# The low parts of the split weight tiles: VectorE and GpSimd together, or VectorE alone

## The chip, the cores and the metric

The kernel runs on one core of a Trainium2 chip. What is compared is the device time of one execution in microseconds (us), as the median of several runs. Besides that there is one profiled execution, whose trace tells when each instruction began and ended on each engine: PE (TensorE matmuls, with PEld for the weight loads that overlap them), DVE (VectorE), ACT (ScalarE), POOL (GpSimd) and SP (SyncE, which here only issues DMAs).

## The reference, cut to what matters

Two layers of a hybrid backbone work on 256 context tokens and 512 latent tokens of width 1024. Each layer normalizes and modulates its input, makes one large input projection, feeds three parallel branches (SSD, gated linear attention GLA, and S5), and ends in an output projection and a residual.

```
u_lat = rmsnorm(h_lat, norm_w[l]) * (1.0 + scale[:, None]) + shift[:, None]
u_ctx = rmsnorm(h_ctx, norm_w[l]) * (1.0 + scale_c) + shift_c
(z_c, xbc_c, dt_c, q_c, k_c, v_c, gg_c, lr_c, u5_c, sg_c) = split_in_proj(u_ctx @ w_in[l])
(z_l, xbc_l, dt_l, q_l, k_l, v_l, gg_l, lr_l, u5_l, sg_l) = split_in_proj(u_lat @ w_in[l])
...
ssd_c, ssd_l = ssd_branch(...)
gla_c, gla_l = gla_branch(...)
s5_c, s5_l = s5_branch(...)
...
y = pr[..., :S5_WIDTH] * jax.nn.sigmoid(pr[..., S5_WIDTH:])      # in s5_branch, after y @ glu_w
```

All of it is in 32-bit floating point. The weight matrices that concern us are `w_in`, `w_out` and `glu_w`.

## The kernel before, in words

A 32-bit product is made of three faster ones. Each operand is split into a high part, rounded to the type `fp32r`, and a low part, which is the operand minus its high part. The matmuls then add high*high, high*low and low*high (`PASSES`). For a weight tile of 128 x 1024 the function `wsplit` does the splitting: a DMA brings the tile into `wr`, ACT copies it with rounding into `wh`, and one `tensor_tensor` with SUB makes `wl = wr - wh`. Each of the three tags has two buffers, so the next tile but one can be loaded only when the subtraction has read `wr`, and its `wh` written only when PE has read the old one. There are 122 weight tiles, two of them 128 x 512 (the `wdl` tile of each layer). They are used by `proj` (input projection; L492 makes the latent columns in a `pl` bank, L494 the context columns in `pc`), by the V projection (L709), by the GLU of S5 (L1026, L1028) and by `out_part` (L1062, L1064).

Which engine makes a low part is set by a counter: each third tile goes to VectorE (`V`), the others to GpSimd (`G`). So VectorE makes 40 and GpSimd 82. The parameter `eng` is given by no caller.

The order of instructions on each engine is not the order of the source. A scheduler simulates the program as it is built and issues each instruction on its engine's queue where its own estimate of times puts it; each queue is then worked off strictly in order. A change to one instruction can therefore move others.

Other places that the text speaks of: `s5_out_map` (L375 to L385 on POOL, matmuls L394, DVE L400 and L401) makes the S5 output maps, 16 per layer, between the projections; L473 on DVE makes the low parts of the normalized input; `carry` (L643 to L646) is the S5 scan on DVE; L830 and L833 finish the GLA branch on DVE and POOL; `conv_tile` (L856, L863, L865 on DVE) is the convolution; L916, L918 and L921 on DVE, with the copies on ACT and L941, L944 and L954 on POOL, are the SSD chunks; L511 on DVE is a gate that also empties a projection's PSUM bank; all ACT instructions have the line of their helper, L121.

Of the kernel before, what the change touches and what calls it, by code (L numbers as in the profile page):

```python
# [8 lines left out]
F32 = mybir.dt.float32  # L9
# [6 lines left out]
ADD, SUB, MUL, MIN, MAX = ALU.add, ALU.subtract, ALU.mult, ALU.min, ALU.max  # L16
# [25 lines left out]
def hybrid_backbone_kernel(  # L42
# [16 lines left out]
    V, S, G, PE = nc.vector, nc.scalar, nc.gpsimd, nc.tensor  # L59
# [9 lines left out]
    def T(tag, shape, bufs, dt=F32):  # L69
        uid[0] += 1  # L70
        return sb.tile(shape, dt, tag=tag, bufs=bufs, name=f"{tag}_{uid[0]}")
# [48 lines left out]
    def act(out, in_, f, **kw):  # L120
        return S.activation(out, in_, f, **kw)  # L121
# [282 lines left out]
        dma(gD[l][gs + 1], gt[48:64])  # L404


    wcount = [0]

    def wsplit(src, n=1024, eng=None):

        wr = T("wr", [128, 1024], 2)[:, :n]
        dma(wr, src)
        wh, wl = (T(t, [128, 1024], 2, F32R)[:, :n] for t in ("wh", "wl"))
        act(wh, wr, AF.Copy)
        wcount[0] += 1
        (eng or (V if wcount[0] % 3 == 0 else G)).tensor_tensor(wl, wr, wh.bitcast(F32), SUB)  # L416
        return wh, wl

    def split(hi, lo, x, eng):
# [56 lines left out]
    def layer(l, u):  # L476
# [5 lines left out]
        def proj(blocks, m=128, ctx_too=True, src=None, early=False):  # L482

            w = wsplit(src if src is not None else wblk[l, blocks], 8 * m)
            p_l, p_c = pl(), pc() if ctx_too else None
            seq = [(k, wi, ui) for k in range(8) for wi, ui in PASSES]
            if early:
                seq.sort(key=lambda a: a[2])
            for n, (k, wi, ui) in enumerate(seq):
                st, sp = n == 0, n == 23  # L490
                lhs = w[wi][:, k * m : (k + 1) * m]
                PE.matmul(p_l[:m], lhs, u[k][:, ui, LC:NT], start=st, stop=sp)  # L492
                if ctx_too:
                    PE.matmul(p_c[:m], lhs, u[k][:, ui, 0:LC], start=st, stop=sp)  # L494
            return p_c, p_l
# [204 lines left out]
        for hb in range(2):  # L700
            ws = [wsplit(wblk[l, BV + 2 * hb + i]) for i in range(2)]
            for c in range(6):
                if c % 3 == 0:
                    e_ = ev()
                p = pl()[:, 0:256]
                n = 0
                for k in range(8):
                    for wi, ui in PASSES:
                        PE.matmul(p, u[k][:, ui, 128 * c : 128 * c + 128],  # L709
                                  ws[k // 4][wi][:, 256 * (k % 4) : 256 * (k % 4) + 256], start=n == 0, stop=n == 23)  # L710
                        n += 1
                act(e_[:, 256 * (c % 3) : 256 * (c % 3) + 256], p, AF.Copy)
                if c % 3 == 2:
                    dma(vD[l][128 * c - 256 : 128 * c + 128, 256 * hb : 256 * hb + 256].rearrange("(c p) v -> p c v", c=3),
                        e_.rearrange("p (c v) -> p c v", c=3))
# [301 lines left out]
        for m in range(4):  # L1017
            wv = wsplit(wglu[l, m])
            pair = []
            for half in range(2):  # L1020
                p_l, p_c = pl(), None if last else pc()
                n = 0
                for k in range(4):
                    for wi, ui in PASSES:
                        lhs = wv[wi][:, (half * 4 + k) * 128 : (half * 4 + k) * 128 + 128]
                        PE.matmul(p_l, lhs, yg5[k][:, ui, LC:NT], start=n == 0, stop=n == 11)  # L1026
                        if not last:
                            PE.matmul(p_c, lhs, yg5[k][:, ui, 0:LC], start=n == 0, stop=n == 11)  # L1028
                        n += 1
                pair.append((p_c, p_l)[-len(cols):])  # L1030

            sg, gt = cv(NT), cv(NT)
            dma(gt[:, t0:NT], sgD[l][128 * m : 128 * m + 128, t0:NT])
            for i, (a, b) in enumerate(cols):
                act(sg[:, a:b], pair[1][i], AF.Tanh, scale=2.0, bias=pcol("glb", 8 * l + 4 + m))
            s3 = sg[:, t0:NT].rearrange("p (t c) -> p t c", t=8)
            V.scalar_tensor_tensor(s3, s3, 1.0, gt[:, t0:NT].rearrange("p (c t) -> p t c", t=8), ADD, MUL)
            for i, (a, b) in enumerate(cols):
                V.scalar_tensor_tensor(sg[:, a:b], pair[0][i], pcol("glb", 8 * l + m), sg[:, a:b], ADD, MUL)
            t = hl()  # L1040
            s3, hi, lo = (a.rearrange("p (c t) -> p c t", t=8) if k else a.rearrange("p (t c) -> p c t", t=8)
                          for k, a in enumerate((sg[:, t0:NT], t[:, 0, t0:NT], t[:, 1, t0:NT])))
            split(hi, lo, s3, G)
            ys5.append(t)
# [215 lines left out]
```

## Time and profile before

| what | value |
|---|---|
| median of 3 runs | 1697.27 us (1695.55 to 1711.04) |
| profiled execution, its own time | 1712.97 us |
| its span from first to last instruction | 1711.3 us |
| granted TensorE clock, mean over the span | 0.901 of full speed |

The profiled execution took 15.7 us more than the median. Sums made from its rows are differences against 1712.97 us, and are carried over to the median of 1697.27 us.

### The profile page before, as it was taken

What the parts mean: (1) busy time and instruction counts of PE and PEld (TensorE: products, weight loads), DVE (VectorE), ACT (ScalarE), POOL (GpSimd) and SP (SyncE); (2) the same over time, 40 slices, a digit from 0 to 9 for tenths busy, and PEclk for the clock granted to TensorE, in tenths of its full rate; (3) what the DMA queues carried; (4) which work ended last, traced back from release to release, by engine and by line L of the source; (5) the groups of instructions that cost most, each with busy time, mean ns of one, the idle gap of its engine ahead of it and who ended that gap; (6) DMA issues with size and microseconds to landing.
All of it is one profiled execution on the core that took longest, in us unless ns stands there. A gap on an engine that the chain in (4) does not pass through costs nothing.

```text
span 1711.3 us, 23539 instructions
## 1 busy us (share of the span) xinstructions
PE 1418.1 (83%) x8536; PEld 1145.2 (67%) x8536; DVE 1168.2 (68%) x1992; ACT 679.9 (40%) x1220; POOL 783.2 (46%) x716
## 2 busy tenths in 40 slices
PE   3867766888989779977779999997889989967886
PEld 2656655777966557755668786886678777745665
DVE  7977558995477567679994127289835986688752
ACT  4312223225342336646553124343345345545442
POOL 3615647632268843445463141164123323656454
PEclk9788987898988889988889999998988999988998
DMA  8474654332543354444455745522363242344542
GB/s 308 124 185 135 178 150 135 93 118 71 176 123 86 100 165 140 142 154 139 128 187 188 282 135 178 189 85 80 111 193 107 64 139 93 119 138 145 184 131 96
DMA packets 139885, 243.55 MB, mean 142 GB/s; under 512 B 31992, under 2 KB 72568, under 8 KB 139768
## 3 DMA queue, kind: packets, MB, share of 16 engines
q1 hardware_dynamic: 139768, 242.04, 45.3%
q8 instruction: 67, 1.10, 0.3%
q14 instruction: 50, 0.41, 0.1%
HBM read 192.81 MB, written 49.18 MB: 141 GB/s over the span
## 4 chain that ended last, share of the span: by engine, by line
PE 25%; DVE 18%; DMA 13%; POOL 6%; issue 4%; ACT 4%; SPq 0%; DVEq 0%; ACTq 0%; POOLq 0%
PE pl L492 7%; PE pl L1062 6%; DMA bA<-acsD 5%; DMA bB<-acsD 3%; PE pc L494 2%; PE pc L1064 2%; DVE xy L863 1%; DMA wr<-in_wblk 1%; ACT bA L121 1%; POOL wl L416 1%; DVE bB L916 1%; DVE bA L916 1%; DVE xy L645 1%; DMA cs<-zD 1%; DVE bA L644 1%
## 5 line engine op out<-in xcount | busy, mean ns | idle before, releaser
L492 PE MATMUL pl<-hl,wh 128*128 128x512 f32 (+1 forms) x1184 | 411.5, 414 | 15.9 <-DVE ev L511 12.3
L416 POOL TENSOR_TENSOR wl<-wr,wh 128x1024 fp32r<-128x1024 f32 (+1 forms) x82 | 210.4, 2566 | 308.5 <-ACT wh L121 284.6
L492 PEld LDWEIGHTS pl<-hl,wh 128*128 128x128 f32 (+1 forms) x1184 | 226.0, 195 | 73.5 <-DVE ev L511 13.6
L492 PE MATMUL pl<-hl,wl 128*128 128x512 f32 (+1 forms) x592 | 243.5, 412 | 20.0 <-POOL wl L416 10.7
L121 ACT ACTIVATE wh<-wr 128x1024 fp32r<-128x1024 f32 (+1 forms) x122 | 127.6, 1047 | 283.7 <-PE pc L1064 69.3
L494 PE MATMUL pc<-hl,wh 128*128 128x256 f32 (+1 forms) x864 | 202.0, 304 | 11.3 <-DVE ev L511 7.2
L494 PEld LDWEIGHTS pc<-hl,wh 128*128 128x128 f32 (+1 forms) x864 | 152.5, 202 | 26.1 <-DVE ev L511 8.7
L492 PEld LDWEIGHTS pl<-hl,wl 128*128 128x128 f32 (+1 forms) x592 | 115.4, 195 | 49.1 <-POOL wl L416 12.0
L494 PE MATMUL pc<-hl,wl 128*128 128x256 f32 (+1 forms) x432 | 128.6, 298 | 0.0
L1062 PE MATMUL pl<-hl,wh 128*128 128x512 f32 x256 | 87.7, 419 | 16.9 <-ACT hl L121 4.6
L394 PE MATMUL pa<-cs 64*32 64x128 f32 x512 | 42.9, 305 | 64.0 <-POOL cs L382 27.3
L494 PEld LDWEIGHTS pc<-hl,wl 128*128 128x128 f32 (+1 forms) x432 | 87.3, 202 | 2.7 <-issue 1.7
L121 ACT ACTIVATE ev<-pl 128x512 f32<-128x512 f32 (+1 forms) x96 | 51.1, 534 | 87.7 <-PE pl L709 43.9
L709 PE MATMUL pl<-wh,hl 128*128 128x256 f32 x384 | 79.6, 307 | 2.6 <-ACT ev L121 2.6
L416 DVE TENSOR_TENSOR wl<-wr,wh 128x1024 fp32r<-128x1024 f32 x40 | 55.4, 1386 | 38.3 <-ACT wh L121 38.1
L121 ACT ACTIVATE bB<-bB 128x512 f32<-128x512 f32 (+4 forms) x40 | 45.7, 1142 | 85.1 <-DMA bB<-acsD 52.3
L394 PEld LDWEIGHTS pa<-cs 64*32 64x32 f32 x512 | 21.5, 115 | 80.6 <-POOL cs L382 28.9
L863 DVE SCALAR_TENSOR_TENSOR xy<-ev,par_sb,xy 128x512 f32<-128x512 f32 (+1 forms) x112 | 74.8, 704 | 0.6
L375 POOL TENSOR_SCALAR cs<-cs 128x32 f32<-128x32 f32 x32 | 20.1, 629 | 118.4 <-DMA cs<-in_s5cb 43.3
L709 PEld LDWEIGHTS pl<-wh,hl 128*128 128x128 f32 x384 | 66.9, 214 | 7.8 <-ACT ev L121 3.8
L1062 PEld LDWEIGHTS pl<-hl,wh 128*128 128x128 f32 x256 | 49.8, 199 | 31.1 <-ACT hl L121 6.7
L709 PE MATMUL pl<-wl,hl 128*128 128x256 f32 x192 | 58.4, 308 | 3.8 <-DVE wl L416 3.8
(483 smaller groups left out, 3604.4 us busy)
## 6 DMA issues: line engine op xcount, KB each, us to landing
wr<-in_wblk SPq DMA_DIRECT2D x80, 512.0 KB
wr<-in_wout SPq DMA_DIRECT2D x32, 512.0 KB
hl<-in_mod_w SPq DMA_DIRECT2D x20, 512.0 KB
bA<-acsD SPq DMA_DIRECT2D x10, 1024.0 KB
bB<-acsD SPq DMA_DIRECT2D x10, 1024.0 KB
clD<-cs SPq DMA_DIRECT2D x64, 128.0 KB
cs<-clD SPq DMA_DIRECT2D x32, 256.0 KB
cs<-in_mod_w SPq DMA_DIRECT2D x16, 512.0 KB
```

Source lines behind the costliest of these rows:

```text
L121: return S.activation(out, in_, f, **kw)
L375: G.tensor_scalar(cn, cb[:, 0:32], -1.0, None, MUL)
L394: PE.matmul(pk[d][32 * gg : 32 * gg + 32], b0[64 * d : 64 * d + 64, a, :], w54[64 * d : 64 * d + 64, a, gg, d : 8 + d, :].rearrange("p k h ...
L416: (eng or (V if wcount[0] % 3 == 0 else G)).tensor_tensor(wl, wr, wh.bitcast(F32), SUB)
L492: PE.matmul(p_l[:m], lhs, u[k][:, ui, LC:NT], start=st, stop=sp)
L494: PE.matmul(p_c[:m], lhs, u[k][:, ui, 0:LC], start=st, stop=sp)
L644: V.tensor_tensor(tr[:, 1, :n], li, src[:, :, ::-1], MUL)
L709: PE.matmul(p, u[k][:, ui, 128 * c : 128 * c + 128], ws[k // 4][wi][:, 256 * (k % 4) : 256 * (k % 4) + 256], start=n == 0, stop=n == 23)
L863: V.scalar_tensor_tensor(ac, raw[:, o + k : o + k + n], pcol("cw", w0 + k), ac, MUL, ADD)
L916: V.scalar_tensor_tensor(rf[:, h, :], rbw[:, h, :], rb[:, ih : ih + 1], rf[:, h, :], SUB, MIN)
L1062: PE.matmul(p_l, lhs, rhs[kk][:, ui, LC - t0 : NT - t0], start=st, stop=sp)
L1064: PE.matmul(p_c, lhs, rhs[kk][:, ui, 0:LC], start=st, stop=sp)
```

## The change

The counter and the `eng` parameter go, and VectorE makes every low part.

```diff
--- before.py
+++ after.py
@@ -404,16 +404,13 @@
-    wcount = [0]
-
-    def wsplit(src, n=1024, eng=None):
+    def wsplit(src, n=1024):
 
         wr = T("wr", [128, 1024], 2)[:, :n]
         dma(wr, src)
         wh, wl = (T(t, [128, 1024], 2, F32R)[:, :n] for t in ("wh", "wl"))
         act(wh, wr, AF.Copy)
-        wcount[0] += 1
-        (eng or (V if wcount[0] % 3 == 0 else G)).tensor_tensor(wl, wr, wh.bitcast(F32), SUB)
+        V.tensor_tensor(wl, wr, wh.bitcast(F32), SUB)
         return wh, wl
```

The file is three lines shorter, so L416 of before is L413 after, and all later lines move by three. In the rows below, the numbers behind a name tell its instances apart and are the same in both kernels. On POOL, at the end of GLA in layer 0, two weight tiles' low parts stood among the instructions of `s5_out_map` (before):

```order
L383 TENSOR_TENSOR cs_2306<-s5p_1800,cs_2306 128x288
L375 TENSOR_SCALAR cs_2333<-cs_2333 128x32
L380 TENSOR_TENSOR cs_2333<-s5p_1800,cs_2333 128x288
L381 TENSOR_TENSOR cs_2333<-s5p_1800,cs_2333 128x288
L416 TENSOR_TENSOR wl_4870<-wr_4867,wh_4869 128x1024
L382 TENSOR_TENSOR cs_2306<-cs_2306 128x288
L383 TENSOR_TENSOR cs_2333<-s5p_1800,cs_2333 128x288
L833 TENSOR_TENSOR m_266_2994<-m_266_2994,bB_2995 128x3072
L382 TENSOR_TENSOR cs_2333<-cs_2333 128x288
L384 TENSOR_TENSOR cs_2306<-s5p_1800,cs_2306 128x288
L416 TENSOR_TENSOR wl_4946<-wr_4943,wh_4945 128x1024
```

On DVE, the first of the two stands after the change behind the GLA norm's large multiply (L827, which was L830) and inside one convolution tile:

```order
L827 SCALAR_TENSOR_TENSOR m_266_2994<-m_266_2994,par_sb,bB_2995 128x3072
L400 TENSOR_TENSOR cs_2090<-cs_2090,pa_2102 64x16
L860 SCALAR_TENSOR_TENSOR bc_4694<-ev_4693,par_sb,bc_4694 128x512
L860 SCALAR_TENSOR_TENSOR bc_4694<-ev_4693,par_sb,bc_4694 128x256
L401 SCALAR_TENSOR_TENSOR cs_2090<-i_96,par_sb,cs_2090 64x16
L413 TENSOR_TENSOR wl_4870<-wr_4867,wh_4869 128x1024
L860 SCALAR_TENSOR_TENSOR bc_4694<-ev_4693,par_sb,bc_4694 128x512
L860 SCALAR_TENSOR_TENSOR bc_4694<-ev_4693,par_sb,bc_4694 128x256
L862 SCALAR_TENSOR_TENSOR bc_4694<-ev_4693,bc_4694 128x512
```

So the subtraction no longer stands behind `s5_out_map` and the GLA gate's product (L833) on POOL; behind it now stand the last taps of the convolution tile.

At the start of layer 0, on DVE, the low parts of the normalized input (L473) are followed before by other small work:

```order
L473 SCALAR_TENSOR_TENSOR hl_457<-xy_141,modp,hl_457 128x512
L345 TENSOR_TENSOR cs_174<-s5p_139,cs_171 128x576
L210 TENSOR_TENSOR modp<-pa_420,par_sb 128x8
L261 COPY bA_484<-bA_484 128x32
L298 TENSOR_TENSOR bA_484<-bA_484 128x32
```

and after the change by the first two weight tiles' subtractions, which stood on POOL with nothing ahead of them but the normalization:

```order
L470 SCALAR_TENSOR_TENSOR hl_457<-xy_141,modp,hl_457 128x512
L345 TENSOR_TENSOR cs_174<-s5p_139,cs_171 128x576
L210 TENSOR_TENSOR modp<-pa_420,par_sb 128x8
L413 TENSOR_TENSOR wl_553<-wr_550,wh_552 128x512
L261 COPY bA_484<-bA_484 128x32
L298 TENSOR_TENSOR bA_484<-bA_484 128x32
L413 TENSOR_TENSOR wl_863<-wr_860,wh_862 128x1024
```

Here the first subtraction has come to stand behind eight of the sixteen L473 and L345, and the other eight L473 stand behind both. Over the whole program all 122 subtractions are on DVE, none on POOL, and the remaining instructions of each engine are the same but for four fewer table loads on ACT.

## Rows read from the trace of the kernel before

**Rows 1.** The page: each engine's busy time, share and instructions.

```profile
PE 1418.1 (83%) x8536; PEld 1145.2 (67%) x8536; DVE 1168.2 (68%) x1992; ACT 679.9 (40%) x1220; POOL 783.2 (46%) x716
```

**Rows 2.** The chain that ended last, by engine.

```profile
PE 25%; DVE 18%; DMA 13%; POOL 6%; issue 4%; ACT 4%; SPq 0%; DVEq 0%; ACTq 0%; POOLq 0%
```

**Rows 3.** Stretches: us; busy PE, PEld, DVE, ACT, POOL; clock, DMA.

```profile
650.00:700.00 50.00, 48.33 (x308) 39.68 (x307) 27.68 (x51) 36.75 (x81) 19.68 (x15) 1.00 0.27 88
950.00:1050.00 100.00, 96.58 (x621) 71.56 (x620) 34.12 (x57) 28.75 (x40) 24.04 (x14) 0.97 0.52 186
1140.00:1210.00 70.00, 56.83 (x338) 49.09 (x337) 69.06 (x93) 27.89 (x36) 28.61 (x16) 0.90 0.30 91
```

**Rows 4.** Line L416, its instructions: duration in ns, least, median, most.

```profile
L416 POOL TENSOR_TENSOR wl<-wr,wh x82: 1290/2400/5506, 46.4 to 1684.5; 128x1024 fp32r<-128x1024 f32 x80, 128x512 fp32r<-128x512 f32 x2
L416 DVE TENSOR_TENSOR wl<-wr,wh x40: 1207/1224/2489, 70.0 to 1673.6; 128x1024 fp32r<-128x1024 f32 x40
```

**Rows 5.** The page's group of L416 on DVE: busy, mean ns, idle before.

```profile
L416 DVE TENSOR_TENSOR wl<-wr,wh 128x1024 fp32r<-128x1024 f32 x40 | 55.4, 1386 | 38.3 <-ACT wh L121 38.1
```

**Rows 6.** Timeline: start, us, what; DVE instructions beside a subtraction on POOL.

```profile
45.85 4.95 DVE L473 SCALAR_TENSOR_TENSOR hl<-xy,modp,hl 128x512 fp32r<-128x512 f32 x3
46.45 3.80 POOL L416 TENSOR_TENSOR wl<-wr,wh 128x512 fp32r<-128x512 f32 x2 [9.23 <-ACT wh L121]
...
326.53 2.36 POOL L416 TENSOR_TENSOR wl<-wr,wh 128x1024 fp32r<-128x1024 f32 x1
326.76 2.94 DVE L646 TENSOR_TENSOR xy<-xy,bA 128x768 f32<-128x768 f32 x1
...
333.97 0.94 DVE L646 TENSOR_TENSOR xy<-xy,bA 128x768 f32<-128x768 f32 x1
...
1539.60 2.38 POOL L416 TENSOR_TENSOR wl<-wr,wh 128x1024 fp32r<-128x1024 f32 x1 [4.21 <-ACT wh L121]
1539.63 0.67 DVE L940 TENSOR_TENSOR bB<-ps,bB 128x512 f32<-128x512 f32 x1
...
1638.39 3.36 POOL L416 TENSOR_TENSOR wl<-wr,wh 128x1024 fp32r<-128x1024 f32 x1
1639.43 2.86 DVE L421 TENSOR_TENSOR bA<-xy,bA 128x512 fp32r<-128x512 f32 x1
```

**Rows 7.** Timeline from 574 to 619 us, one engine after the other.

```profile
586.10 2.52 POOL L416 TENSOR_TENSOR wl<-wr,wh 128x1024 fp32r<-128x1024 f32 x1
...
598.18 2.37 POOL L416 TENSOR_TENSOR wl<-wr,wh 128x1024 fp32r<-128x1024 f32 x1
...
574.47 1.04 ACT L121 ACTIVATE wh<-wr 128x1024 fp32r<-128x1024 f32 x1
...
574.60 3.42 DVE L830 SCALAR_TENSOR_TENSOR m<-m,par_sb,bB 128x3072 f32<-128x3072 f32 x1 [3.60 <-ACT bB L121]
...
588.67 0.80 PE L492 MATMUL pl<-hl,wl 128*128 128x512 f32 x1 [9.02 <-POOL wl L416]
...
601.84 6.30 SPq L412 DMA_DIRECT2D wr<-in_wblk  x2
...
618.31 1.01 PEld L394 LDWEIGHTS pa<-cs 64*32 64x32 f32 x16 [12.09 <-ACT cs L121]
```

**Rows 8.** Who waited for whom: us in total, times, longest.

```profile
PE pl L492 <- POOL wl L416: 10.7, 3, 9.0
```

**Rows 9.** Timeline of the start of layer 0: PE, then DVE.

```profile
47.80 0.69 PE L492 MATMUL pl<-hl,wl 128*64 128x512 f32 x1
...
50.72 0.74 DVE L345 TENSOR_TENSOR cs<-s5p,cs 128x576 f32<-128x576 f32 x1
...
53.28 0.74 DVE L473 SCALAR_TENSOR_TENSOR hl<-xy,modp,hl 128x512 fp32r<-128x512 f32 x1
```

**Rows 10.** Timeline: DVE's two longest waits before a subtraction.

```profile
600.57 1.25 DVE L416 TENSOR_TENSOR wl<-wr,wh 128x1024 fp32r<-128x1024 f32 x1 [14.15 <-ACT wh L121]
...
686.73 1.23 DVE L416 TENSOR_TENSOR wl<-wr,wh 128x1024 fp32r<-128x1024 f32 x1 [7.04 <-ACT wh L121]
```

## The prediction

> **What bounds the kernel now.** I read the page's totals first. PE is busy for 1418.1 us of the span and DVE for 1168.2, POOL only for 783.2 [rows 1]. A reader might stop there: DVE is the second busiest engine, POOL has room, and the change loads the one and empties the other. So I read the chain that ended last: PE stands in it with 25% of the span, DVE with 18%, POOL with 6% [rows 2]. No engine bounds the whole; the limit changes by stage, as the table of stretches shows. Around the output projection of layer 0 (950 to 1050 us) PE is busy for 96.58 of 100 us and DVE for 34.12. In the S5 scan of layer 1 (1140 to 1210) it is DVE, 69.06 of 70 us, while PE idles for 13 [rows 3]. What a moved subtraction is worth depends on which of these two kinds of stretch it lies in.
>
> **The cost on DVE, and what it frees there.** The change moves 82 subtractions. On POOL one takes 2.40 us in the median, on DVE 1.224 [rows 4]; the mean on DVE is 1.386, since some were held up [rows 5]. So DVE is given 82 x 1.224 = 100 us at the least, and 82 x 1.386 = 114 us if the new ones are held up like the old (two are half as wide; I leave that out). Taken alone that is 9 to 10% more work on an engine that bounds some stages.
>
> But a subtraction on POOL already costs DVE time. At 326.53 POOL begins one of 2.36 us; DVE's scan instruction L646, begun at 326.76, takes 2.94 us, where the same instruction takes 0.94 at 333.97. It ends 0.81 us after POOL's: it lay still until POOL was done. At 1539.63 DVE's L940, which reads one operand from PSUM, takes 0.67 us beside a POOL subtraction; that one isn't held [rows 6]. I went through all 82 and took, for each DVE instruction beside one, what it lasted above the value that a fifth of its own kind stay below: 52 of the 82 held up DVE by more than 0.3 us, and all together they cost it 98 us. The first and the last of these pairs stand in [rows 6].
>
> The Trainium skill has a rule for this (SBUF — State Buffer, section "SBUF: two separate sides"): VectorE and GpSimd share a pair of SBUF ports, whichever starts first holds it for its whole instruction, and a VectorE instruction with two SBUF inputs is among those that block and are blocked. The held L646 and the free L940 agree with it. The rule cuts both ways: the new subtractions on DVE will hold POOL's reads too. A sum that knew no hold would leave out the 98 us and, with half of them on the path as below, end 49 us higher.
>
> So in total DVE gains nothing: 100 to 114 us come and 98 go. By place it is different. The 52 lie where DVE is full of SBUF work, which are mostly the stretches that it bounds; there each costs 1.386 in place of 98 / 52 = 1.89 us, so 52 x 0.50 = 26 us go. The other 30 lie where POOL's subtraction held up nobody, and 30 x 1.386 = 42 us come onto a DVE that is idle two thirds of the time beside PE, as from 950 to 1050 [rows 3]; without that cover they would cost up to those 42 us. How much of the 26 is on the path? Not all, since PE and DMAs end other waits there. I take half: **-13 us** (0 to -26).
>
> **What POOL's queue no longer holds.** PE's L492 waits for a POOL subtraction for 10.7 us in all, and 9.0 of it is one wait [rows 8]. The rows around it show what it is. ACT had written that `wh` by 575.5, but POOL's subtraction began only at 586.10, because `s5_out_map` stood ahead of it in the queue; PE stood still for 9.02 us. The next one came at 598.18, behind more maps and L833. A `wr` buffer is free only after the subtraction, so SP issues further weight loads from 601.84 on [rows 7]. The tiles' rounding stands in ACT's queue, and at 618.31 a weight load has waited 12.09 us for an ACT copy [rows 7]; for 11.8 of these neither a matmul nor a load ran.
>
> After the change the first of these stands on DVE behind L827 (L830 of before) and four taps of a convolution tile, as the order shows. In the trace L830 ended at 578.0 [rows 7], so the subtraction would be done by about 581 to 582 where POOL ended it at 588.6. PE began to wait at 579.7, and would gain about 7 to 8 of its 9.0 us. Then the second wait shrinks as well, but surely not all of it, because DMAs for the SSD decay are in ACT's queue at the same place. I take 8 and half of 11.8: **-14 us** (-7 to -21). The rest of POOL's queue moves up behind 210 us less work; I count nothing for that, and set against it that POOL's reads are held by DVE's new subtractions.
>
> The shorter subtraction itself, 1.2 us less from `wh` to `wl`, is worth nothing more: beyond the 9.0 us this PE line waited 1.7 us in all for POOL's subtractions [rows 8], since PE works on the other tile meanwhile. What would show if that cover were gone is 1.2 us for each tile.
>
> **The first weight.** At 47.80 PE uses the first low part, made on POOL from 46.45 [rows 6, 9]. In the new order it stands behind eight L473 and L345, which ended at 51.5 in the trace [rows 9]. Three of the L473 took 4.95 us beside POOL's first two subtractions, where a wide one alone takes 0.74 [rows 6, 9]; that hold of about 3 us goes, so DVE gets there at 48.5 and is done by about 49.2. PE gets it 1.5 us later, or 4.5 without that relief, early in a stage where it soon waits for other things. I take **+1 us** (0 to +4.5).
>
> **New waits on DVE.** A subtraction in DVE's queue whose `wh` isn't there yet stops everything behind it: gates that empty PSUM (L511), convolutions, SSD decays, and PE and ACT behind these. The 40 of before waited 38.1 us for ACT [rows 5]. At that rate 82 more make 82 x 38.1 / 40 = 78 us. What of it reaches the end is unknown. The longest, 14.15 us, lies at 600.57, in the very stretch where POOL's queue was late, and is an effect of that lateness; the second, 7.04 us at 686.73 [rows 10], lies where PE is busy for 48.33 of 50 us [rows 3]. I take a tenth: **+8 us** (0 to +39, half of it).
>
> **The sum:** -13 - 14 + 1 + 8 = **-18 us**, from 1712.97 to about 1695 us for the profiled execution, and carried over to the median 1697.27 - 18 = **1679 us**, 1.1% less. From end to end of the terms it goes from -26 - 21 = -47 (1650 us) to 0 - 7 + 4.5 + 39 = +36 (1734 us). About 1% is what a measurement of this kernel can tell from no change (its three runs lie 0.9% apart), and the forecast lies just beyond it.
>
> **The rivals.**
> *Nothing reaches the end.* The released DVE time is taken by waits that end last anyway, and the order, moved in many places, gives the gain of POOL's queue back: the terms -13 and -14 shrink to what the new waits cost, -9 + 1 + 8 = 0, so 1697 us. For it: DMAs hold 13% of the chain [rows 2], and DVE's total doesn't fall. Against it: the 9.02 us at 588.67 is PE's own wait [rows 7].
> *DVE's queue stands (slower).* The subtraction waits on DVE for ACT's `wh`, with L511, L863 or an SSD decay behind it. Two thirds of the 78 us worked out above make 52: 52 + 1 - 13 - 14 = +26, so 1723 us. It is slower by over 1% from a share of 55% on (43 us). For it: the order is made from estimates, and ACT's copies wait for PE to free a buffer. Against it: the two longest waits of before, 21 of 38 us, didn't hold PE by themselves.
> *The hold gives back everything.* All 26 us of the held 52, and all 21 us of POOL's queue, without new waits: 1697 - 47 = 1650 us. This is how it goes if the held instructions are always those that PE waits for. For it stands the S5 scan, where DVE is full and PE idle [rows 3]; against it the SSD chunks, which share their chain with DMAs and ACT.
> The lock rule cited above would make this one come true wherever DVE is full of instructions with two SBUF inputs.
> *The change doesn't do what it says.* The order shows 122 subtractions on DVE and none on POOL; this gets no chance.
>
> **How the numbers follow.** The forecast gets 0.51, of which 0.36 is faster by over 1% and 0.15 within it; nothing reaching the end 0.20 (all within 1%); DVE's queue 0.19 (slower); everything given back 0.10 (faster). That makes 0.46 faster, 0.35 the same, 0.19 slower. The range of 8 in 10 goes from 1648, about the full gain, to 1722, where half of the slower case is left out.
>
> **What the changed profile should show.** L413 on DVE 122 times, 1.22 us in the median and near 1.39 in the mean; DVE busy between 1165 and 1190 us, no higher; POOL busy near 575 us; the scan's L643 (L646 of before) and the SSD's L913 and L915 (L916 and L918) shorter in the mean; no wait of PE for a low part over 5 us around 580 us; and waits of DVE's subtractions for ACT of about 100 us in all, mostly beside a busy PE. The prediction is wrong if DVE's busy time rises by 50 us or more (the holds then passed to other POOL work), or if PE's idle time grows behind DVE instructions that follow a subtraction.

## The result, and the profile after

The changed kernel takes 1682.1 us (median of 9 runs, 1678.08 to 1689.88) where the kernel before takes 1701.66 (9 runs now; the 1697.27 above was the median of the first 3): a ratio of 0.9878 with the interval [0.9856, 0.9899], 1.0 to 1.4% faster. The profiled execution took 1689.88 us, its span is 1688.2.

First the page of the changed kernel: the engines' totals, the chain by engine, and the group of the subtraction (L413 now, L416 before).

```profile
PE 1416.3 (84%) x8536; PEld 1145.0 (68%) x8536; DVE 1169.3 (69%) x2074; ACT 677.3 (40%) x1216; POOL 598.7 (35%) x634
...
PE 29%; DVE 14%; DMA 13%; ACT 5%; issue 4%; POOL 4%; SPq 1%; DVEq 0%; ACTq 0%; POOLq 0%
...
L413 DVE TENSOR_TENSOR wl<-wr,wh 128x1024 fp32r<-128x1024 f32 (+1 forms) x122 | 168.2, 1379 | 98.3 <-ACT wh L121 97.4
```

DVE has 82 more instructions than in [rows 1] and is busy for 1.1 us more. The subtractions cost it 168.2 us in place of 55.4 [rows 5], and everything else on it got shorter by 112 us. POOL is busy for 184.5 us less. Its 82 subtractions took 210.4 us before, so what stayed on it got 26 us longer:

```profile
L416 POOL TENSOR_TENSOR wl<-wr,wh 128x1024 fp32r<-128x1024 f32 (+1 forms) x82 | 210.4, 2566 | 308.5 <-ACT wh L121 284.6
```

Where DVE's 112 us came from is seen in the groups by line. Of before, the decays of the SSD (L916, L918) and one line of the S5 scan (L646):

```profile
L918 DVE SCALAR_TENSOR_TENSOR bA<-bA,dts 128x128 f32<-128x128 f32 x80 | 49.6, 675 | 3.5 <-ACT bA L121 3.3
...
L916 DVE SCALAR_TENSOR_TENSOR bB<-bB,dts 128x128 f32<-128x128 f32 x80 | 40.4, 566 | 0.0
...
L646 DVE TENSOR_TENSOR xy<-xy,bA 128x64 f32<-128x64 f32 (+3 forms) x50 | 36.2, 723 | 1.0
```

The same three of the changed kernel, three lines higher in the code:

```profile
L915 DVE SCALAR_TENSOR_TENSOR bA<-bA,dts 128x128 f32<-128x128 f32 x80 | 35.2, 492 | 1.0 <-ACT bA L121 0.9
L913 DVE SCALAR_TENSOR_TENSOR bB<-bB,dts 128x128 f32<-128x128 f32 x80 | 32.6, 457 | 1.4 <-ACT bB L121 1.4
L643 DVE TENSOR_TENSOR xy<-xy,bA 128x64 f32<-128x64 f32 (+3 forms) x50 | 32.0, 640 | 0.7
```

Their number and shapes are the same; the mean falls by 11 to 27%. These are among the instructions that a subtraction on POOL used to stop.

What DVE and PE wait for at the subtraction, of the whole changed run (us in total, times, longest):

```profile
DVE wl L413 <- ACT wh L121: 97.4, 35, 13.8
...
PE pl L489 <- DVE wl L413: 14.0, 7, 6.9
```

DVE's waits for ACT are the 100 us that were expected. No wait of PE for a low part near 580 us is left: its 9.02 us of [rows 7] are gone.

So far all looks as forecast. The question is in which place of the program the 23 us between the two spans lie. I cut each run at the last instruction of four lines: the S5 scan (L646 of before), the convolutions (L865), the SSD decays (L921) and the residual at a layer's end (L1076). The view of stretches (us; busy PE, PEld, DVE, ACT, POOL with counts; clock, DMA) for the kernel before, layer 0 as a whole and then the four stages of layer 1:

```profile
0.00:1023.10 1023.10, 825.82 (x5298) 666.88 (x5302) 701.84 (x1263) 378.70 (x704) 508.07 (x492) 0.89 0.49 152
1023.10:1231.20 208.10, 185.80 (x1125) 152.94 (x1118) 155.14 (x240) 74.27 (x119) 65.90 (x49) 0.93 0.41 131
1231.20:1442.30 211.10, 192.37 (x1151) 166.03 (x1149) 141.57 (x238) 102.98 (x150) 68.16 (x87) 0.90 0.38 115
1442.30:1608.20 165.90, 135.06 (x645) 99.52 (x646) 123.32 (x205) 84.93 (x199) 92.86 (x64) 0.91 0.44 141
1608.20:1711.30 103.10, 79.01 (x328) 59.80 (x327) 46.37 (x49) 39.06 (x51) 48.23 (x26) 0.91 0.40 130
```

And for the changed kernel, cut at the same instructions:

```profile
0.00:1023.50 1023.50, 837.68 (x5298) 675.10 (x5302) 706.61 (x1305) 377.17 (x702) 420.80 (x450) 0.89 0.50 152
1023.50:1232.70 209.20, 194.81 (x1193) 160.78 (x1186) 158.20 (x262) 78.84 (x126) 37.86 (x41) 0.96 0.43 139
1232.70:1429.10 196.40, 174.58 (x1078) 150.34 (x1077) 131.05 (x239) 95.84 (x140) 34.12 (x72) 0.91 0.39 116
1429.10:1592.30 163.20, 131.10 (x646) 97.89 (x645) 125.02 (x215) 86.13 (x201) 75.27 (x56) 0.92 0.46 144
1592.30:1688.20 95.90, 78.09 (x335) 60.93 (x333) 48.39 (x55) 39.33 (x50) 30.67 (x17) 0.92 0.42 137
```

Layer 0, where the prediction had put 14 of its 18 us by name, ends at the same time: 1023.1 and 1023.5. All of it comes from layer 1: 688.2 us before, 664.7 after. There the S5 scan is no shorter (208.1 and 209.2), but in the same time DVE issues 262 instructions in place of 240, and PE 1193 matmuls in place of 1125. What PE has done by then is missing from the next stage, which takes 196.4 us in place of 211.1. The last stage gives 7.2 more.

### The profile page after: what moved, and what is told of

Same layout as the page of the kernel before. It is cut to its first block, busy times and chain, and to the rows that moved or that the text cites. A ratio compares the mean times of both kernels' runs of the same rounds, so it can differ in the third digit from the quotient of the medians.

```text
span 1688.2 us, 23555 instructions
## 1 busy us (share of the span) xinstructions
PE 1416.3 (84%) x8536; PEld 1145.0 (68%) x8536; DVE 1169.3 (69%) x2074; ACT 677.3 (40%) x1216; POOL 598.7 (35%) x634
## 4 chain that ended last, share of the span: by engine, by line
PE 29%; DVE 14%; DMA 13%; ACT 5%; issue 4%; POOL 4%; SPq 1%; DVEq 0%; ACTq 0%; POOLq 0%
PE pl L489 8%; PE pl L1059 6%; DMA bB<-acsD 5%; DMA bA<-acsD 5%; PE pc L491 3%; DVE wl L413 3%; PE pc L1061 2%; ACT bB L121 1%; DVE xy L860 1%; PE pl L706 1%; ACT bA L121 1%; DVE bc L860 1%; DMA cs<-in_s5cb 1%; PE pa L204 1%; PE pl L1023 1%
## 5 line engine op out<-in xcount | busy, mean ns | idle before, releaser
L489 PE MATMUL pl<-hl,wh 128*128 128x512 f32 (+1 forms) x1184 | 407.3, 412 | 4.2 <-ACT wh L121 1.9
L413 DVE TENSOR_TENSOR wl<-wr,wh 128x1024 fp32r<-128x1024 f32 (+1 forms) x122 | 168.2, 1379 | 98.3 <-ACT wh L121 97.4
L491 PE MATMUL pc<-hl,wh 128*128 128x256 f32 (+1 forms) x864 | 197.9, 305 | 2.6 <-ACT ev L121 1.2
L1059 PE MATMUL pl<-hl,wh 128*128 128x512 f32 x256 | 92.8, 436 | 25.2 <-ACT cv L121 8.6
L121 ACT ACTIVATE ev<-pl 128x512 f32<-128x512 f32 (+1 forms) x96 | 51.2, 534 | 94.8 <-PE pl L706 31.0
L394 PE MATMUL pa<-cs 64*32 64x128 f32 x512 | 41.5, 303 | 53.6 <-POOL cs L382 23.2
L375 POOL TENSOR_SCALAR cs<-cs 128x32 f32<-128x32 f32 x32 | 16.7, 523 | 181.6 <-DMA cs<-in_s5cb 94.7
L860 DVE SCALAR_TENSOR_TENSOR xy<-ev,par_sb,xy 128x256 f32<-128x256 f32 (+1 forms) x112 | 70.5, 672 | 0.7
L394 PEld LDWEIGHTS pa<-cs 64*32 64x32 f32 x512 | 21.2, 114 | 71.0 <-POOL cs L382 26.2
L1023 PE MATMUL pl<-hl,wh 128*128 128x512 f32 x128 | 48.8, 456 | 11.2 <-ACT cv L121 11.0
```

Of the source, the lines that this page charges most:

```text
L375: G.tensor_scalar(cn, cb[:, 0:32], -1.0, None, MUL)
L394: PE.matmul(pk[d][32 * gg : 32 * gg + 32], b0[64 * d : 64 * d + 64, a, :], w54[64 * d : 64 * d + 64, a, gg, d : 8 + d, :].rearrange("p k h ...
L413: V.tensor_tensor(wl, wr, wh.bitcast(F32), SUB)
L860: V.scalar_tensor_tensor(ac, raw[:, o + k : o + k + n], pcol("cw", w0 + k), ac, MUL, ADD)
L1059: PE.matmul(p_l, lhs, rhs[kk][:, ui, LC - t0 : NT - t0], start=st, stop=sp)
```

## The experiments

Three theories stood after this. *Holds*: POOL's subtractions stop DVE's instructions, and in layer 1 that is on the path. *Lateness*: the low part (or the buffer) came late from POOL's queue. *Order*: the scheduler merely wrote a luckier order. All kernels are the kernel before with the choice of the engine in L416 edited, each compared with the kernel before on the same chip (medians of 1704.57 to 1705.78 us there). Layer 0 has tiles 1 to 61 and layer 1 tiles 62 to 122; in each layer the first 33 go up to the convolutions, the other 28 are gates, GLU and output. Unless said otherwise, the edit replaces the condition for VectorE in

```diff
-        (eng or (V if wcount[0] % 3 == 0 else G)).tensor_tensor(wl, wr, wh.bitcast(F32), SUB)
```

### By layer, and the choice of the third

```diff
e1_layer0: + (V if wcount[0] <= 61 or wcount[0] % 3 == 0 else G)
e2_layer1: + (V if wcount[0] > 61 or wcount[0] % 3 == 0 else G)
e3_phase1: + (V if wcount[0] % 3 == 1 else G)
e4_phase2: + (V if wcount[0] % 3 == 2 else G)
```

All of layer 0 on DVE:

> VectorE makes every low part in layer 0 alone; layer 1 keeps the split of one in three. By the prediction's terms (the POOL queue around 580 us, -14, and half of the DVE holds) layer 0 should bring about -18 of the -20 us. By the trace of the changed kernel, where the first instructions of layer 1 begin no earlier than before, it brings about 0 (within 5 us). If the gain is only a matter of how the scheduler's order happens to fall, it can be anything between -15 and +15.

All of layer 1 on DVE:

> VectorE makes every low part in layer 1 alone; layer 0 keeps the split. By the trace of the changed kernel the whole gain comes from here: about -20 us (ratio 0.987 to 0.99). By the prediction's terms about -5 us. If the two layers don't act on each other, this and the run with layer 0 alone add up to the ratio 0.988.

The same split with another third of the tiles on DVE, first one, then the other:

> The same split of one low part in three on VectorE, but the first, fourth, seventh ... tile in place of the third, sixth, ninth. The load on each engine is that of before to within one tile. If the time follows from the load (holds on DVE and the number of subtractions on POOL), it is that of before within 5 us. If the order of the scheduler decides, it differs from before by as much as the change did (10 to 25 us, either way).

> The same with the second, fifth, eighth ... tile on VectorE. Expected like the run before it: within 5 us of the kernel before if the load decides, 10 to 25 us off either way if the order does. With it there are three draws of the same split.

Measured: layer 0 alone 1708.54 us, ratio 1.001 [0.9994, 1.0027]: nothing. Layer 1 alone 1684.17 us, 0.9874 [0.9856, 0.9893]: the whole effect of the change. The other thirds: 1729.47 us, 1.0115 [1.0086, 1.0145], and 1708.4 us, 1.0007 [0.9986, 1.0027]. Of the first of these two only the time is used. So another order at the same split can cost 1.1%, and the order cannot be ruled out by the size of the gain alone. What bears on it comes with the table of stages further below.

### Two tiles at 580 us

```diff
e8_two_tiles: + (V if wcount[0] in (31, 32) or wcount[0] % 3 == 0 else G)
```

> The kernel before, but the two tiles around 580 to 600 us of layer 0 (the 31st and 32nd) are subtracted by DVE; all others stay. The prediction's term for POOL's queue at this place: 7 to 21 us less, a time of about 1692 where the kernel before has 1706. Theory that layer 0's gain there is taken by the SSD stage behind it: the 9 us wait of PE near 580 us goes, layer 0 still ends within 4 us of 1023, and the time is within 4 us of the kernel before. Theory of the order: layer 0 ends anywhere from 1010 to 1047.

Measured: 1714.8 us, 1.0066 [1.0041, 1.0091]: slower, and layer 0 ends at 1036.8; neither of the first two sums foresaw it, and the range given for the order holds it. The timeline of this kernel at the place (start, us, what, wait before it), PE, POOL and DVE:

```profile
589.37 0.63 PE L394 MATMUL pa<-cs 64*32 64x128 f32 x2 [8.55 <-POOL cs L382]
...
584.76 3.80 POOL L381 TENSOR_TENSOR cs<-s5p,cs 128x288 f32<-128x288 f32 x1
588.53 0.79 POOL L382 TENSOR_TENSOR cs<-cs 128x288 f32<-128x288 f32 x1
...
579.96 1.23 DVE L416 TENSOR_TENSOR wl<-wr,wh 128x1024 fp32r<-128x1024 f32 x1
```

The low part is now there at 581.2 (DVE began it at 579.96), and PE still stands still until 589.37. It waits for `cs`, which the S5 output map makes on POOL. The order of PE at this place, kernel before (-) and this one (+), shows how that came about:

```
 L494 MATMUL pc_66<-hl_467,wh_4793 128x256 x2
+L394 MATMUL pa_2317<-cs_2306 32x128
 L494 MATMUL pc_66<-hl_467,wl_4794 128x256
...
 L492 MATMUL pl_4873<-hl_462,wl_4870 128x512
-L394 MATMUL pa_2317<-cs_2306 32x128
-L394 MATMUL pa_2318<-cs_2306 32x128
```

The scheduler put L394 forward, ahead of the matmuls that read the low part, and PE works its queue in order. `cs` was not earlier: in the kernel before, POOL ran this L382 from 588.58, right behind the subtraction; now it runs it from 588.53 without a subtraction ahead. The map's table came 2.6 us later (L375 began at 577.46 and not at 574.82), and L381 took 3.80 us in place of 1.15. The kernel before:

```profile
574.82 3.35 POOL L375 TENSOR_SCALAR cs<-cs 128x32 f32<-128x32 f32 x1 [6.01 <-DMA cs<-in_s5cb]
...
584.99 1.15 POOL L381 TENSOR_TENSOR cs<-s5p,cs 128x288 f32<-128x288 f32 x1
...
588.58 0.79 POOL L382 TENSOR_TENSOR cs<-cs 128x288 f32<-128x288 f32 x1
```

The matmuls of the two tiles, whose low part lies ready, stand behind L394. The changed kernel has a wait of the same kind at the same place:

```profile
590.40 0.64 PE L394 MATMUL pa<-cs 64*32 64x128 f32 x4 [7.43 <-POOL cs L382]
```

Why this kernel is 9 us slower rather than equal isn't settled: its SSD of layer 0 takes 200.1 us in place of 189.0, in another order.

### The hold by itself

```diff
e7_hold:
+        (V if wcount[0] > 61 or wcount[0] % 3 == 0 else G).tensor_tensor(wl, wr, wh.bitcast(F32), SUB)
+        if wcount[0] > 61 and wcount[0] % 3:
+            hh = wh.bitcast(F32)
+            G.tensor_tensor(wr, hh, hh, SUB)
e15_release: the same, but
+            hh = wh[:, 0:16].bitcast(F32)
+            G.tensor_tensor(wr[:, 0:16], hh, hh, SUB)
```

> As the kernel with all low parts of layer 1 on VectorE (1684 us in the first set of runs, against 1706 for the kernel before), but for the 41 tiles that moved there POOL subtracts wh from itself, too, into the tile's wr, which nobody reads any more: the subtraction's traffic on POOL comes back, the useful low part still comes from DVE. Theory of the holds (layer 1 gains because POOL's subtractions no longer stop DVE's instructions): DVE's instructions are held by about 45 us in layer 1 again, layer 1 lasts 683 to 690 us as with the old split, the time is 1700 to 1708. Theory of lateness (layer 1 gains because the low part comes earlier): the low part still comes from DVE, layer 1 lasts 660 to 668, the time is 1682 to 1690. Theory of the order (the planned order of layer 1 merely happens to be better with all on DVE): no link with either, layer 1 anywhere between 660 and 700, and DVE's holds needn't show in the stages that grow.

> The kernel with the 41 repeated POOL subtractions, but these now cover 16 columns in place of 1024: wr and wh are still given free by POOL's queue, and hardly anything is read or written by POOL. The run with the full width took 1714.8 us where the kernel before took 1705.3, with layer 1 at 694.0 us; without any repeated subtraction layer 1 took 660.0. Theory of the holds: what brought the time back was POOL's full-width traffic, so it stays away now: layer 1 at 660 to 670 us, the time 1682 to 1692. Theory of lateness: it was the buffers that POOL's queue gave free late: layer 1 at 684 to 696, the time 1703 to 1715.

Measured: with the full width 1714.78 us, 1.006 [1.0039, 1.008]; with 16 columns 1684.22 us, 0.988 [0.986, 0.99]. The first is beyond the 1700 to 1708 us that the holds were to give, the second within its 1682 to 1692. The two have the same instructions on DVE, and in both POOL's queue gives `wr` and `wh` free; they differ in the width of 41 POOL instructions, and by 30.6 us. The stages of layer 1, full width:

```profile
1015.70:1229.10 213.40, 192.68 (x1169) 158.94 (x1162) 167.22 (x261) 77.22 (x122) 67.96 (x52) 0.96 0.41 133
1229.10:1436.70 207.60, 182.93 (x1109) 157.00 (x1109) 149.01 (x241) 94.44 (x142) 54.53 (x84) 0.90 0.37 111
1436.70:1604.30 167.60, 134.71 (x634) 99.40 (x633) 135.49 (x215) 84.10 (x198) 92.85 (x63) 0.89 0.44 137
1604.30:1709.70 105.40, 81.66 (x337) 62.35 (x336) 54.89 (x57) 40.24 (x52) 47.05 (x27) 0.89 0.39 132
```

and 16 columns:

```profile
1014.20:1223.50 209.30, 195.25 (x1193) 161.37 (x1186) 158.28 (x263) 79.26 (x126) 42.26 (x54) 0.96 0.44 139
1223.50:1424.40 200.90, 181.58 (x1079) 156.80 (x1078) 130.53 (x239) 95.63 (x140) 41.15 (x82) 0.88 0.38 113
1424.40:1585.40 161.00, 131.72 (x646) 98.13 (x646) 125.13 (x216) 86.11 (x201) 80.86 (x65) 0.93 0.45 145
1585.40:1681.50 96.10, 77.84 (x334) 60.74 (x332) 49.80 (x55) 38.58 (x50) 32.71 (x25) 0.92 0.42 140
```

DVE is busy for 506.6 us in the four stages of the first and for 463.7 in those of the second, with the same work; layer 1 takes 694.0 and 667.3 us, and 21 of the 27 us between them are idle time of PE. So lateness by itself doesn't explain the gain: in the first kernel the low part comes from DVE and the layer is long, and in the second the buffers wait for POOL's queue and it is short.

The holds are shown, but their price at the end is not shown apart from the order. The scheduler wrote the two kernels differently: of the 709 instructions that DVE has in layer 1 besides the subtractions, 492 stand in the same sequence, while the kernel of 16 columns shares 673 with that of layer 1 alone. Where at least ten in a row are the same (276 of the 709), DVE is held for 25.3 and 12.3 us (the measure is the prediction's: what an instruction lasts above the value that a fifth of its kind stay below), and these rows last 299.5 and 299.6 us. For the holds speaks the chain that ended last: followed back through layer 1, it has 39.5 us of held DVE time in the first kernel and 17.7 in the second. It has 43 to 55 in the four kernels of the table below whose layer 1 is in the order of before, and 17 to 21 in the three with that of after. A stretch of the first kernel shows the holds one by one, POOL and then DVE:

```profile
1178.18 2.63 POOL L768 TENSOR_TENSOR bB<-bB 128x768 f32<-128x768 f32 x1 [2.04 <-DMA wr<-in_wblk]
1180.77 1.88 POOL L419 TENSOR_TENSOR wr<-wh 128x1024 f32<-128x1024 f32 x1
...
1179.01 1.87 DVE L646 TENSOR_TENSOR bA<-cs,xy 128x64 f32<-128x64 f32 x1
1180.81 1.92 DVE L647 TENSOR_TENSOR bA<-cs,xy 128x64 f32<-128x64 f32 x1
...
1184.84 0.22 DVE L646 TENSOR_TENSOR bA<-cs,xy 128x64 f32<-128x64 f32 x1
```

An instruction of the scan over 64 columns takes 0.22 us when POOL is quiet, 1.92 beside L419 (the repeated subtraction) and 1.87 beside another POOL instruction; each ends within 0.1 us of POOL's. In the kernel of 16 columns, POOL's L419 has a median of 0.22 us (least, median and most in ns), and there is next to nothing to wait for:

```profile
L419 POOL TENSOR_TENSOR wr<-wh x41: 207/216/1922, 1006.9 to 1657.0; 128x16 f32<-128x16 f32 x41
```

The Trainium skill has this as a rule (SBUF — State Buffer, section "SBUF: two separate sides"): the pair of ports is an exclusive lock for a whole instruction, not a share of bandwidth. These rows agree: the DVE instruction of 0.22 us pays for the rest of POOL's.

### The two halves of layer 1, and more on POOL

```diff
e9_to_conv: + (V if 62 <= wcount[0] <= 94 or wcount[0] % 3 == 0 else G)
e10_from_bz: + (V if wcount[0] > 94 or wcount[0] % 3 == 0 else G)
e16_all_pool1: + (V if wcount[0] <= 61 and wcount[0] % 3 == 0 else G)
```

> Of layer 1 only the weight tiles up to the convolutions (62nd to 94th, 22 moved) go to DVE. Theory of the holds: the subtractions of POOL up to the end of the convolutions held DVE by 37 us of layer 1's 47.5 in the trace of before, and the gain of the kernel with all of layer 1 on DVE lay to 18 of 28 us before that point; so 16 to 19 us less than before, 1686 to 1690 where before has 1706, and from the carry to the end of the convolutions the stretch falls from 211 to about 193 us. Theory of the order: no such sum; the parts needn't add up, either part can be at 0 or at more than the whole.

> The other part of layer 1: only the tiles from the gates of the SSD on (95th to 122nd, 19 moved) go to DVE. Theory of the holds: 10.5 us of holds go there, and 5 to 10 us of the time, so 1696 to 1701 where before has 1706; the stretch up to the convolutions stays at 211 us. Theory of the order: as for its other part, the sum of the two needn't be the whole (21 us).

> The opposite dose: in layer 1 POOL makes all 61 low parts, also the 20 that DVE has in the kernel before; layer 0 keeps the old split, and its order with it. Theory of the holds: 41 subtractions taken from POOL brought 24 to 28 us, 0.6 each; 20 more on POOL cost 12 us, in the stretch from the carry to the convolutions and after the SSD; layer 1 lasts 695 to 705 us in place of 688, the time is about 1717 where before has 1705. Theory of the order: no link with the number, layer 1 can be shorter than 688 as well. A reader who counts only DVE's own time would expect 20 times 1.39 = 28 us less work on DVE and a layer 1 no longer than 688.

Measured: 1692.35 us, 0.9932 [0.991, 0.9955]; 1689.67 us, 0.9913 [0.989, 0.9935]; and with all 61 on POOL 1731.03 us, 1.015 [1.0119, 1.0182]. The stages of all runs but e3_phase1 (us; the ends as above), and the time of layer 1 in which PE is idle:

| kernel | subtractions on POOL in layer 1 | layer 0 ends | S5 scan | to convolutions | SSD | rest | layer 1 | PE idle |
|---|---|---|---|---|---|---|---|---|
| before | 41 | 1023.1 | 208.1 | 211.1 | 165.9 | 103.1 | 688.2 | 95.9 |
| e1_layer0 | 41 | 1027.5 | 207.8 | 211.0 | 166.4 | 101.8 | 686.9 | 98.5 |
| e4_phase2 | 40 | 1012.7 | 213.3 | 204.3 | 162.7 | 104.5 | 684.7 | 103.2 |
| e8_two_tiles | 41 | 1036.8 | 208.2 | 209.7 | 164.8 | 102.9 | 685.6 | 97.1 |
| e14_to_conv0 (below) | 41 | 1016.6 | 207.5 | 208.8 | 164.9 | 104.2 | 685.4 | 94.2 |
| e9_to_conv | 19, in the last two stages | 1019.5 | 209.1 | 194.6 | 166.8 | 100.8 | 671.4 | 88.1 |
| e10_from_bz | 22, in the first two | 1016.0 | 207.9 | 206.5 | 160.4 | 95.6 | 670.5 | 89.9 |
| after | 0 | 1023.5 | 209.2 | 196.4 | 163.2 | 95.9 | 664.7 | 86.1 |
| e2_layer1 | 0 | 1019.6 | 209.1 | 192.3 | 162.3 | 96.2 | 660.0 | 81.7 |
| e13_from_bz0 (below) | 0 | 1019.4 | 209.2 | 191.3 | 162.1 | 96.4 | 659.0 | 82.8 |
| e15_release | 41 of 16 columns | 1014.2 | 209.2 | 200.9 | 161.0 | 96.2 | 667.3 | 80.9 |
| e7_hold | 41 repeated | 1015.7 | 213.4 | 207.6 | 167.5 | 105.4 | 694.0 | 102.0 |
| e16_all_pool1 | 61 | 1020.1 | 214.6 | 232.7 | 163.6 | 100.1 | 711.0 | 107.4 |

The half up to the convolutions shortens the stretch that it lies in by 16.5 us and the last two stages by 1.4 only; the other half shortens the last two by 13.0 and the stretch before them by 4.6. So each half acts where its subtractions lie. The sums of the holds came true in part: layer 1 of the first half is 16.8 us shorter (16 to 19 expected), but its time fell by 13.0 us only; the second half brought 17.7 us in the layer and 15.7 in the time, where 5 to 10 were expected; and 13.0 and 15.7 are more than the 21.6 of the whole. The halves don't test the order either. The order of DVE changes only where subtractions moved: besides these, the first 447 of the 709 instructions of e10_from_bz stand as before, and the first 445 of e9_to_conv as in e2_layer1.

Layer 1 takes 684.7 to 688.2 us in all five kernels with 40 or 41 subtractions on POOL, and 659.0 to 664.7 in all three with none. These are fewer draws of the order than they seem: DVE's layer 1 stands in one order in before, e1, e8 and (but for one instruction) e14, and in another in after, e2 and e13. Against a merely lucky order speaks the last column. Over eight different orders PE's idle time goes with the number of full-width subtractions on POOL: 81 to 86 us with none, 88 and 90 with 19 and 22, 94 to 103 with 40 or 41, 107 with 61. That the scheduler doesn't write a better order because POOL has less to do isn't shown; no run holds the order fixed and changes the width alone.

The opposite dose was priced too low: 23 us more and not 12. Half of the 23 is idle time of PE, the other half are longer matmuls (603.6 us in place of 592.2; the last section has the reason). The waits of PE in layer 1 of that kernel (us in total, times, longest) show what came to the holds:

```profile
PE pl L492 <- POOL wl L416: 8.4, 3, 5.2
PE pl L709 <- POOL wl L416: 6.2, 1, 6.2
PE pl L1062 <- POOL wl L416: 5.6, 3, 3.1
```

In layer 1 PE waits 20.2 us for a low part, where it waited 10.7 before (for both engines' together). So lateness is real once POOL's queue holds all of them; at the old split it wasn't what layer 1 paid for (in e7_hold PE waits 7.3 us for low parts there). DVE's busy time in that layer, 455.3 us, is the lowest of all kernels in the table, and the layer the longest: counting DVE's own work would have got the sign wrong.

### Layer 0 in parts

```diff
e13_from_bz0: + (V if wcount[0] > 33 or wcount[0] % 3 == 0 else G)
e14_to_conv0: + (V if wcount[0] <= 33 or wcount[0] % 3 == 0 else G)
```

> All low parts on DVE from the gates of layer 0's SSD on (the 34th tile); up to the convolutions of layer 0 (the first 33 tiles) the old split. In the five profiles whose layer 0 has the order of before, that layer ends between 1015.7 and 1023.1 us. In the two with all of layer 0 on DVE the S5 stage takes 13 to 19 us more than in these, the way to the end of the convolutions 4 more, the SSD 6 more, the end of the layer 21 less. Theory that each stage gains or loses by its own subtractions: the loss of the first stages stays away, the 15 us of the last two are kept, layer 0 ends near 1004, layer 1 takes 660 to 665: a time of 1662 to 1670. Theory of the order: layer 0 ends anywhere from 1010 to 1047, the time is 1675 or more.

> The counterpart in layer 0: only its first 33 tiles (up to the convolutions) go to DVE, all others as before. Theory that each stage gains or loses by its own subtractions: the carry of layer 0's S5 comes 13 to 19 us later and the end of the convolutions 18 to 22, with DVE's waits for DMAs in the S5 stage at 70 us in place of 55; layer 0 ends near 1038, the time is about 1722 to 1726 where before has 1705. Theory of the order: layer 0 ends anywhere from 1010 to 1047. The prediction's term for POOL's queue in this part of layer 0 would give 1684 to 1698.

Measured: 1688.23 us, 0.9906 [0.9886, 0.9927], and 1703.74 us, 0.9993 [0.9975, 1.0012]. Both of my sums for layer 0 failed. In the first, the SSD of layer 0 ended at 843.9 us in place of 863.5, as hoped, and the layer ended at 1019.4 all the same: its last stage took 175.5 us in place of 159.6. In the second, the S5 scan ended at 420.9 and the convolutions at 687.7, late as expected (406.7 and 674.5 before), and the layer ended at 1016.6, with a last stage of 126.4. PE does the same 5298 matmuls in the layer, and only their place changes: by stage it is busy for 300.1, 222.6, 149.3 and 153.9 us before, and for 326.9, 224.2, 163.5 and 120.5 in the second. A stage that ends late there has done more of PE's work; its end says nothing of what was lost. With PE full at the end of the layer [rows 3], what counts is PE's idle time in all of the layer and how long its matmuls take.

## Why the prediction came out as it did

The total was right, 1679 forecast and 1682.1 measured (18 us less forecast, 19.6 less measured), and so were all the signs that it named but one: L413 122 times with 1.225 us in the median and 1.379 in the mean, DVE at 1169.3 us, shorter scan and SSD instructions, waits for ACT of 97.4 us (84.5 of them beside a busy PE), no wait for a low part near 580. POOL's 598.7 us were forecast near 575: what remained on it was held by DVE's new subtractions for more than I had counted (by the measure of the holds it loses 52.5 us beside them, and lost 13.7 beside the 40 of before). But that the total fits is luck: it is the sum of two wrong halves, as the runs by layer show, and 13.7 of the 23.5 us that layer 1 gained in the profile came through TensorE's clock, for which the sum had no term.

**The held instructions (-13, 0 to -26).** That POOL's subtractions stop DVE's instructions is shown; what it is worth was off. By the measure of the prediction DVE loses 95.8 us in layer 1 before, 50.5 after, 94.0 with the repeated subtraction and 51.2 with the 16 columns. Of the 98 us that the prediction found, 47.5 lay in layer 1, and nearly all of them went; the layer became 23.5 us shorter in the profile, and 21.6 in the time of the run with layer 1 alone. Together with the new waits, for which I had set +8, this half was forecast at -5 for the whole kernel and came out at -22 from layer 1 alone.

Two steps failed. I set each hold off against the subtraction's own 1.386 us on DVE, and took half of the rest. By that sum layer 1's share of the net 26 us is about 13, so even the whole of it isn't 22. The runs show the two on different scales: with POOL's traffic kept, 41 subtractions more on DVE (57 us of its time at 1.386) cost 9.5 us against the kernel before, and taking the traffic away brought 30.6 (both with another order, so neither is a pure price). And 13.7 of the layer's 23.5 us are shorter matmuls, as the last section shows.

**POOL's queue around 574 to 619 us (-14, -7 to -21).** Wrong. The wait went and another took its place at once, for `cs` from the same POOL queue, 8.55 us with the two tiles moved and 7.43 in the changed kernel. The step that failed is "PE began to wait at 579.7, and would gain about 7 to 8 of its 9.0 us": I had read what PE waited for, but not what PE's new order would have it wait for next, though L394, which reads what those same POOL instructions write, stood a few rows behind. Layer 0 alone gave +2.8 us, which is nothing within its interval, where the terms for POOL's queue and the first weight made -13. The first weight itself went as forecast: DVE began it at 48.67, and PE used it at 49.40 in place of 47.80.

**In layer 0 the holds gave nothing either.** DVE loses 160.9 us there before and 123.8 after, 37 less. PE idles for 185.8 us in place of 197.3, but its same matmuls took 837.7 us in place of 825.8, as the first rows of the two tables of stretches show. The lower idle time is no clear gain, since executions of one and the same order differ by as much: seven kernels of the table (before, e2, e7, e9, e10, e15, e16) have one and the same order of DVE in layer 0, and in their profiles PE idles there for 186 to 197 us, its matmuls take 821 to 832, and the layer ends at 1014.2 to 1023.1. It is not that DVE had room in this layer: in its S5 scan, too, it was as good as full before:

```profile
320.00:390.00 70.00, 59.68 (x360) 51.00 (x359) 67.61 (x128) 11.52 (x19) 22.50 (x23) 0.90 0.30 95
```

Why 37 us of holds less bring nothing here is open.

**New waits on DVE (+8, 0 to +39).** They came as counted, 97.4 us in 35 waits; in layer 1 they rose from 14.9 to 57.6 us, and the layer became shorter all the same. Over the whole program PE waits 24.3 us before, and 23.2 after, for a subtraction on DVE or one of the three DVE instructions behind it, so the sign of a slower DVE queue didn't show. Their own price wasn't measured apart from the holds: it is in the -22.

**What the S5 scan of layer 0 paid.** One cost had no term: SP's queue. In layer 0 up to 420 us SP waits at weight loads for 46.5 us in all before and for 97.1 after, of which the view puts 33.1 down to the subtraction on DVE and 45.1 to the gate (L508, which was L511); the scan's own loads stand behind them, and DVE's waits for transfers there rise from 55 to 70 us (of 10.2 us more before, at the same line L361, the view names no cause). That the one causes the other was only argued; at the end of the layer it doesn't show.

Of the rivals, "the hold gives back everything" was nearest for layer 1, and "nothing reaches the end" for layer 0. No version beat the changed kernel: all on DVE in layer 1 alone (0.9874) and from the gates of layer 0 on (0.9906) lie within its interval or beside it.

## What to carry to other kernels

An operation moved off a helper engine is worth what it did to its neighbours: look for instructions of one kind that take three times as long beside it, and price the move by stages, since 45 us of holds less went with a layer shorter by 24 us, and 37 less in the other layer with nothing, though DVE is as good as full in the scans of both (67.61 of 70 us there, and 69.06 of 70 in layer 1 [rows 3]). Before a wait is counted as gain, find the next thing that the waiting engine needs and ask whether the same queue makes it. To tell a hold from a late result, repeat the suspect operation at full and at small width after the result is already there, and compare the order of the two kernels before the difference is called a price.

## What the runs showed that was not expected

PE's busy time for the same matmuls isn't constant, and it decided as much as the idle time. In layer 1 it adds up to 592.2 us before and 578.6 after (the four stages above), so 13.7 of the 23.5 us gained are shorter matmuls and 9.8 are less idling. In layer 0 it goes the other way: 11.5 us less idling, 11.9 us more busy time.

The mean granted clock hides the reason, since it counts PE's idle time too: it is 0.89 in layer 0 of both, and 0.92 and 0.94 from 1040 to 1660 us. The trace's record of the granted clock, laid over the matmuls, shows it. In layer 1 PE is busy for 86.0 us at the lower of its two levels (1.2 and 2.4 GHz) before and for 58.9 after, in layer 0 for 153.1 and 180.4 (the first 23 us have no record). Half of this time and the time at the upper level make 549.3 and 549.1 us in layer 1, and 742.3 in layer 0 of both. So the work is the same, and only the share of it that fell into low stretches differs.

In layer 1 this goes with the kernel: 72 to 86 us at the lower level in the four profiles with the order of before, 55 to 60 in the three with that of after. In layer 0 the seven profiles of one order have 149 to 174 us, so 180 is little beyond what executions differ by. What keeps the clock up in layer 1 wasn't tried.
